# Finishing the key searches of an expert layer during its first sixteen expert pairs, in a scratch row shared with their activations

## The chip, the cores and the metric

The kernel runs on one core of a Trainium2 chip. A core has a matrix engine (TensorE, PE in the profile), three elementwise engines (VectorE or DVE, ScalarE or ACT, GpSimd or POOL) and SyncE (SP), which here issues loads. The metric is the device time of one execution in microseconds.

## The reference, cut to what matters

The model is two two-layer blocks on 256 tokens of width 1024. Each layer of the first block ends in an expert layer (`peer_ffn`) with 128 x 128 experts, and the change lies there alone; it is computed twice. For each token, 8 heads score 2 x 128 keys, the best 16 of each half are combined, and the best 16 of the 256 sums pick the experts:

```python
q = (xt @ wq).reshape(T, PEER_HEADS, 2, PEER_HALF)
s = jnp.einsum('thpd,hpkd->thpk', q, subkeys).astype(F32)
s1, i1 = lax.top_k(s[:, :, 0], PEER_TOPK)
s2, i2 = lax.top_k(s[:, :, 1], PEER_TOPK)
cand = (s1[..., :, None] + s2[..., None, :]).reshape(T, PEER_HEADS, PEER_TOPK * PEER_TOPK)
...
top_s, pos = lax.top_k(cand, PEER_TOPK)
idx = jnp.take_along_axis(cand_idx, pos, axis=-1)
gate = jax.nn.softmax(top_s, axis=-1)
...
act = jax.nn.gelu(jnp.einsum('td,thkd->thk', xb, ub).astype(F32), approximate=False)
return jnp.einsum('thk,thkd->td', (gb * act).astype(vb.dtype), vb)
```

## The kernel before

**Tiling.** The 256 tokens are two tiles of 128 (`tt` = 0, 1). There are 16 rows of 128 keys (`c` = 0 to 15: 8 heads, 2 halves). The kernel doesn't gather experts: it computes all 128 x 128 activations densely, 128 experts (a unit `c`) at a time, then multiplies them by gates that are zero except for the chosen experts.

**A unit.** `unit` (line 284) loads 512 KB of weights on SP's queue, ScalarE casts the high part `whi` (line 277), VectorE subtracts for the low part `wlo` (line 279), and `fm_unit` (line 302) runs 24 matmuls: high by high, high by low of the tokens, low by high. There are 4 buffers of raw weights, 3 of `whi`, 2 of `wlo`. Two units share one of four large PSUM banks; `divide` (line 444, VectorE) scales the bank into SBUF.

**The stages of `peer`**, in program order:

1. The scores stage: `peer_q` makes queries of 16 units in 8 pairs. After each pair `scores` scales them, runs 8 matmuls against the keys (line 1016), copies the scores to `s`, and traces the searches of these two key rows for both token tiles (32 in a layer).
2. A search (`top_keys`, lines 1031 to 1035, all on VectorE): the best 8 of 128 (MAX8), their indices (a load and FIND_INDEX8), a copy `w` without them (a load and MATCH_REPLACE8), the next best 8, and their indices. Only the last three steps touch `w`, a tile with one buffer.
3. The activations: `u_pair(c)` for c = 0, 2, ... 126 runs two units of `peer_u`, scales them and takes the Gelu on ScalarE (line 1051), into one of three tiles `H`: c < 48, 48 to 111, from 112. The second of these takes the one buffer of tag `late` over from `X`, which holds queries, scores, keys and the scratch space of `top_experts`.
4. `top_experts` (lines 1135 to 1208, almost all VectorE): from the best keys `v` and `ix` to expert indices and gates. It is traced after the pair c = 46 and ahead of the pair c = 48.
5. `gate_block` n (lines 1053 to 1076, 32 of them, 8 tokens each) is traced after the pair c = 48 + 2n: one-hot products on VectorE, 16 matmuls, and two multiplications into `H` (line 1074). Buffers of the one-hots allow two blocks at a time.
6. `peer_v`: the gated activations times the second weights (line 1117).

**What sets the order.** A planner writes each engine's queue before the run. An instruction's number is its place in the program, and `later(n)` adds n to it; among the instructions that are ready by the planner's clock, an engine's queue takes the lowest number first. In the run each queue is worked off in that order. A tile gets a buffer of its tag when its first writer is placed, and gives it back after its last reader. In `later(10000)` the searches have a number behind everything else of the layer, so they fill whatever time VectorE has. The transposes of `top_experts` are numbered as of pair c = 34.

Of the kernel before, what the change touches and what calls it, by code (L numbers as in the profile page):

```python
# [9 lines left out]
F32 = mybir.dt.float32  # L10
# [5 lines left out]
AF = mybir.ActivationFunctionType  # L16
# [5 lines left out]
P = 128  # L22
T = 256
NT = 2
# [180 lines left out]
class Kern:  # L205
# [771 lines left out]
    def peer(self, l):  # L977
        nc = self.nc
        TOP = 8
        with ExitStack() as es:  # L980
# [11 lines left out]
            s = X[:, 4096:8192].rearrange("p (t c k) -> p t c k", t=NT, k=P)  # L992
# [8 lines left out]
            with self.pool("peer_x") as px, ExitStack() as ek:  # L1001
                pk = ek.enter_context(self.pool("peer_k"))
                xT, _, divide = self.turned(self.h, f"norm_ffn{l}", px, "xT")

                raw = self.wr.tile([P, 1024], F32, tag="wraw", name="wraw")
                nc.sync.dma_start(raw, self.d("c_keys"))
                nc.vector.tensor_copy(keys, raw.rearrange("p (k t) -> p k t", t=TOP))
                nc.sync.dma_start(sk, self.d(f"peer_k{l}").rearrange("p a b -> p (a b)"))

                def scores(j, ps, m):  # L1010
                    divide(q[:, j:j + 2], ps)
                    pss = self.bank([P, NT, 2, P])
                    for n in range(2):
                        for tt in range(NT):
                            c = j + n
                            nc.tensor.matmul(pss[:, tt, n], q[:, c, tt * P:tt * P + P], sk[:, c * P:c * P + P],
                                             start=True, stop=True)
                    nc.scalar.copy(s[:, :, j:j + 2], pss)
                    with self.later(10000):
                        for tt in range(NT):  # L1020
                            for c in range(j, j + 2):
                                top_keys(tt, c)


                LOW = -3.0e38
                v = [pk.tile([P, 16, 16], F32, name=f"v{tt}") for tt in range(NT)]
                ix = [pk.tile([P, 16, 16], U32, name=f"ix{tt}") for tt in range(NT)]

                def top_keys(tt, c):
                    src, w = s[:, tt, c], pk.tile([P, P], F32, tag="w", name="w")  # L1030
                    nc.vector.max(v[tt][:, c, 0:8], src)
                    nc.vector.max_index(ix[tt][:, c, 0:8], v[tt][:, c, 0:8], src)
                    nc.vector.match_replace(w, v[tt][:, c, 0:8], src, LOW)
                    nc.vector.max(v[tt][:, c, 8:16], w)
                    nc.vector.max_index(ix[tt][:, c, 8:16], v[tt][:, c, 8:16], w)
                self.fm_proj(xT, f"peer_q{l}", range(16), scores)
                U = self.d(f"peer_u{l}")

                def u_pair(c):
                    if c == EARLY:  # L1040
                        H_.append(big.tile([P, 64, T], F32, tag="late", name="H"))
                    if c == 112:
                        H_.append(big.tile([P, 16, T], F32, tag="last", name="H"))
                    ps = self.bank([P, 2, T], True)
                    for j in range(2):
                        hi, lo = self.unit(U[c + j])
                        self.fm_unit(ps[:, j], hi, lo, xT)
                    i = (c >= EARLY) + (c >= 112)
                    hv = H_[i][:, c - FROM[i]:c - FROM[i] + 2]
                    divide(hv, ps)  # L1050
                    nc.scalar.activation(hv, hv, AF.Gelu)  # L1051

                def gate_block(oh, n):

                    t0 = n * TOP
                    bc = lambda a: a[:, None, t0:t0 + TOP].to_broadcast([P, P, TOP])
                    o2, og = hot[:, n % 2, 0], hot[:, n % 2, 2:4]

                    o1 = hot[:, n % 2, 1].rearrange("p k t -> p (k t)").rearrange("p (a k b) -> p a k b", a=4, b=2)
                    nc.vector.tensor_tensor(o2, keys, bc(i2T), op=ALU.is_equal)  # L1060
                    i1 = i1T[:, t0:t0 + TOP].rearrange("p (a b) -> p a b", b=2)
                    nc.vector.tensor_tensor(o1, keys[:, None, :, 0:2].to_broadcast([P, 4, P, 2]),
                                            i1[:, :, None, :].to_broadcast([P, 4, P, 2]), op=ALU.is_equal)
                    for k in range(2):
                        nc.vector.tensor_tensor(og[:, k], o2, bc(gT[:, k]), op=ALU.mult)  # L1065
                    late = oh.tile([P, P - EARLY, TOP], F32, tag="late", name="late")
                    for b in range(0, TOP, 4):
                        ps = self.bank([P, 4, P])
                        for t in range(4):
                            for k in range(2):  # L1070
                                nc.tensor.matmul(ps[:, t], og[:, k, :, b + t], o1[:, (b + t) // 2, :, t % 2], start=k == 0, stop=k == 1)
                        ps = ps.rearrange("p t c -> p c t")
                        hv = H_[0][:, :, t0 + b:t0 + b + 4]
                        nc.vector.scalar_tensor_tensor(hv, ps[:, 0:EARLY], 1.0 / GS, hv, op0=ALU.mult, op1=ALU.mult)
                        nc.scalar.activation(late[:, :, b:b + 4], ps[:, EARLY:], AF.Copy, scale=1.0 / GS)
                    nc.scalar.dma_start(G[n].rearrange("p (c t) -> p c t", t=TOP), late)

                for c in range(0, EARLY, 2):
                    if c == 34:
                        at = self.tc.cur_priority  # L1080
                    u_pair(c)
                self.top_experts(v, ix, X[:, 0:4096], pk, i1T, i2T, gT, at)
                ek.close()
                with self.pool("peer_oh", 2) as oh:
                    n = 0
                    for c in range(EARLY, 128, 2):
                        u_pair(c)
                        while n < T // TOP and 2 * n < c + 2 - EARLY:
                            gate_block(oh, n)
                            n += 1  # L1090
# [771 lines left out]
```

## Time and profile before

| | us |
|---|---|
| median of 3 runs | 3558.74 (3556.2 to 3559.95) |
| the profiled execution | 3559.58 |
| its span, first to last instruction | 3557.8 |
| TensorE busy | 3475.5 (98%) |
| VectorE busy | 2472.9 (70%) |
| ScalarE busy | 1780.6 (50%) |

Times in a profile count from the span's start. In the first expert layer the scores stage runs from about 357 to 414, the activations to 819; in the second they are some 1085 us later. An engine is busy while an instruction of it is being worked on; a matmul's end is modelled, and TensorE's matmuls overlap each other, so a full TensorE row means that it did not wait, not that it is at its peak. An arrow in a row names what ended the idle time before an instruction.

### The profile page before, as it was taken

What the parts mean: (1) busy time and instruction counts of PE and PEld (TensorE: products, weight loads), DVE (VectorE), ACT (ScalarE), POOL (GpSimd) and SP (SyncE); (2) the same over time, 40 slices, a digit from 0 to 9 for tenths busy, and PEclk for the clock granted to TensorE, in tenths of its full rate; (3) what the DMA queues carried; (4) which work ended last, traced back from release to release, by engine and by line L of the source; (5) the groups of instructions that cost most, each with busy time, mean ns of one, the idle gap of its engine ahead of it and who ended that gap; (6) DMA issues with size and microseconds to landing.
All of it is one profiled execution on the core that took longest, in us unless ns stands there. A gap on an engine that the chain in (4) does not pass through costs nothing. (4 is left out here: it accounts for less than half of the span.)

```text
span 3557.8 us, 59377 instructions
## 1 busy us (share of the span) xinstructions
PE 3475.5 (98%) x23428; PEld 3153.5 (89%) x23428; DVE 2472.9 (70%) x4292; ACT 1780.6 (50%) x2670; POOL 73.8 (2%) x93
## 2 busy tenths in 40 slices
PE   8999999999999999999999999999999999999898
PEld 8888999998888888999998888898898898987797
DVE  7655998977655755899987655665765665657664
ACT  5644454554444854445554444544523544444543
POOL 0000000000000000000000000000001000000000
PEclk9999999999999999999999999999998999999999
DMA  4444556668665544556667756556502455553355
GB/s 159 154 139 151 156 184 196 202 199 288 206 189 189 177 135 148 162 182 189 202 203 262 235 188 189 175 185 193 160 20 77 148 195 176 184 199 115 115 185 163
DMA packets 176832, 620.57 MB, mean 174 GB/s; under 512 B 19868, under 2 KB 20636, under 8 KB 175784
## 3 DMA queue, kind: packets, MB, share of 16 engines
q1 hardware_dynamic: 164000, 584.00, 51.9%
q10 hardware_dynamic: 12552, 32.78, 2.5%
q8 instruction: 183, 3.00, 0.3%
q14 instruction: 97, 0.79, 0.1%
HBM read 594.68 MB, written 22.02 MB: 173 GB/s over the span
## 5 line engine op out<-in xcount | busy, mean ns | idle before, releaser
L279 DVE TENSOR_TENSOR wlo<-wraw,whi 128x1024 fp32r<-128x1024 f32 x1058 | 1290.9, 1221 | 589.8 <-PE ps L1117 249.4
L277 ACT CAST whi<-wraw 128x1024 fp32r<-128x1024 f32 x1058 | 1108.4, 1050 | 1108.5 <-PE ps L302 380.5
L302 PE MATMUL ps<-xT_hi,whi 128*128 128x256 f32 x4432 | 651.1, 284 | 2.9 <-ACT xT_hi L393 2.9
L302 PE MATMUL ps<-xT_hi,wlo 128*128 128x256 f32 x4432 | 645.5, 283 | 5.9 <-DVE wlo L279 5.8
L302 PE MATMUL ps<-xT_lo,whi 128*128 128x256 f32 x4432 | 649.5, 284 | 1.1 <-DVE xT_lo L394 0.8
L302 PEld LDWEIGHTS ps<-xT_hi,wlo 128*128 128x128 f32 x4432 | 576.9, 189 | 9.9 <-DVE wlo L279 8.4
L302 PEld LDWEIGHTS ps<-xT_hi,whi 128*128 128x128 f32 x4432 | 577.5, 189 | 6.3 <-ACT xT_hi L393 5.0
L302 PEld LDWEIGHTS ps<-xT_lo,whi 128*128 128x128 f32 x4432 | 577.7, 189 | 3.5 <-DVE xT_lo L394 1.7
L1117 PE MATMUL ps<-whi,gh 128*128 128x512 f32 x2048 | 520.4, 395 | 1.1 <-DVE gh L1110 1.0
L1117 PEld LDWEIGHTS ps<-whi,gh 128*128 128x128 f32 x2048 | 384.4, 188 | 94.5 <-DVE gh L1110 2.8
L1117 PE MATMUL ps<-wlo,gh 128*128 128x512 f32 x1024 | 280.6, 395 | 0.0
L1117 PEld LDWEIGHTS ps<-wlo,gh 128*128 128x128 f32 x1024 | 192.6, 188 | 45.9
L1051 ACT ACTIVATE H<-H 128x512 f32<-128x512 f32 x128 | 81.1, 633 | 139.8 <-DVE H L444 139.5
L444 DVE TENSOR_TENSOR H<-ps,row 128x512 f32<-128x512 f32 x128 | 88.1, 688 | 73.8 <-PE ps L302 73.8
L290 PE MATMUL ps<-whi,aT_hi 128*128 128x512 f32 x352 | 138.9, 395 | 0.0
L292 PE MATMUL ps<-whi,aT_lo 128*128 128x512 f32 x352 | 138.9, 395 | 0.0
L291 PE MATMUL ps<-wlo,aT_hi 128*128 128x512 f32 x352 | 138.8, 394 | 0.0
L444 DVE TENSOR_TENSOR gu<-ps,row 128x512 f32<-128x512 f32 x88 | 60.9, 692 | 109.3 <-PE ps L302 109.3
L1110 DVE TENSOR_TENSOR gh<-H,gh 128x256 fp32r<-128x256 f32 x256 | 106.9, 418 | 1.9 <-ACT gh L1109 1.6
L1109 ACT CAST gh<-H 128x256 fp32r<-128x256 f32 x256 | 102.5, 401 | 0.0
L1065 DVE TENSOR_TENSOR hot<-hot,gT 128x1024 f16<-128x1024 f16 x128 | 82.2, 681 | 0.0
L292 PEld LDWEIGHTS ps<-whi,aT_lo 128*128 128x128 f32 x352 | 66.3, 188 | 15.5
(636 smaller groups left out, 3995.1 us busy)
## 6 DMA issues: line engine op xcount, KB each, us to landing
wraw<-in_peer_u_dram SPq DMA_DIRECT2D x256, 512.0 KB, 3.7
wraw<-in_peer_v_dram SPq DMA_DIRECT2D x256, 512.0 KB, 4.2
wraw<-in_ff_g_dram SPq DMA_DIRECT2D x88, 512.0 KB, 3.7
wraw<-in_ff_u_dram SPq DMA_DIRECT2D x88, 512.0 KB, 3.3
wraw<-in_ff_d_dram SPq DMA_DIRECT2D x88, 512.0 KB, 4.2
G<-late ACTq DMA_DIRECT2D x64, 320.0 KB, 3.8
g<-G SPq DMA_DIRECT2D x64, 320.0 KB, 5.1
wraw<-in_peer_q_dram SPq DMA_DIRECT2D x32, 512.0 KB, 3.6
```

Of the source, the lines that this page charges most:

```text
L277: nc.scalar.copy(hi, src)
L279: nc.vector.tensor_sub(lo, src, hi.bitcast(F32))
L290: mm(out, a[0], b[0], start=start, stop=False)
L291: mm(out, a[0], b[1], start=False, stop=False)
L292: mm(out, a[1], b[0], start=False, stop=stop)
L302: self.nc.tensor.matmul(out, w[n][0][:, k * P:k * P + P], w[n][1][:, k], start=i == 0, stop=i == 3 * kc - 1)
L444: return dst, lambda tt: r[:, tt:tt + 1], lambda out, ps: nc.vector.tensor_tensor(out, ps, row.to_broadcast([P, ps.shape[1], T]), op=ALU.mult)
L1051: nc.scalar.activation(hv, hv, AF.Gelu)
L1065: nc.vector.tensor_tensor(og[:, k], o2, bc(gT[:, k]), op=ALU.mult)
L1109: nc.scalar.copy(gh, src)
L1110: nc.vector.tensor_sub(gl, src, gh.bitcast(F32))
L1117: nc.tensor.matmul(acc[tt][nb], a[:, tt * P:tt * P + P], w[:, nb * 512:nb * 512 + 512], start=c == 0 and w is hi and a is gh, stop=c == 12 ...
```

## The change

The searches are no longer traced in `scores` with `later(10000)`. They are traced after the pair c for c = 0, 2, ... 30 (key row c // 2, both token tiles) with `later(100)`, which is a little under two pairs' worth of numbers. The scratch tile is twice as wide (both token tiles side by side), and in these sixteen pairs the second half of the activation passes through a tile of the same tag: scaled into `g`, Gelu from `g` into `H`. So `scale` and Gelu are each two instructions of half the width. The tag `w` still has one buffer; in program order its users are g of pair 0, searches 0, g of pair 2, searches 1, and so on.

```diff
                     nc.scalar.copy(s[:, :, j:j + 2], pss)
-                    with self.later(10000):
-                        for tt in range(NT):
-                            for c in range(j, j + 2):
-                                top_keys(tt, c)
...
-                def top_keys(tt, c):
-                    src, w = s[:, tt, c], pk.tile([P, P], F32, tag="w", name="w")
+                def scratch_():
+                    return pk.tile([P, 1, T], F32, tag="w", name="w")
+
+                def top_keys(tt, c, w):
+                    src = s[:, tt, c]
...
-                    divide(hv, ps)
-                    nc.scalar.activation(hv, hv, AF.Gelu)
+
+                    if c < 32:
+                        g = scratch_()
+                        divide(hv[:, 0:1], ps[:, 0:1])
+                        divide(g, ps[:, 1:2])
+                        nc.scalar.activation(hv[:, 0:1], hv[:, 0:1], AF.Gelu)
+                        nc.scalar.activation(hv[:, 1:2], g, AF.Gelu)
+                    else:
+                        divide(hv, ps)
+                        nc.scalar.activation(hv, hv, AF.Gelu)
...
                     u_pair(c)
+                    if c < 32:
+                        w = scratch_()
+                        with self.later(100):
+                            for tt in range(NT):
+                                top_keys(tt, c // 2, w[:, 0, tt * P:tt * P + P])
                 self.top_experts(v, ix, X[:, 0:4096], pk, i1T, i2T, gT, at)
```

## Rows read from the trace of the kernel before

**Rows 1.** The page, busy time and share of the span of each engine.

```profile
PE 3475.5 (98%) x23428; PEld 3153.5 (89%) x23428; DVE 2472.9 (70%) x4292; ACT 1780.6 (50%) x2670; POOL 73.8 (2%) x93
```

**Rows 2.** Stretches: us; busy time (instructions) per engine; clock; DMA share; GB/s.

```profile
357.50:414.50 57.00, 53.49 (x438) 51.95 (x437) 53.37 (x223) 21.05 (x24) 0.00 (x0) 1.00 0.48 148
431.00:543.00 112.00, 110.59 (x920) 109.36 (x919) 108.49 (x265) 55.42 (x64) 0.00 (x0) 1.00 0.58 180
543.00:560.00 17.00, 17.00 (x145) 17.00 (x145) 13.19 (x17) 8.08 (x10) 0.00 (x0) 1.00 0.60 188
560.00:775.00 215.00, 215.00 (x2016) 213.67 (x2015) 193.97 (x277) 110.10 (x158) 0.00 (x0) 1.00 0.66 202
775.00:819.00 44.00, 44.00 (x374) 44.00 (x373) 23.00 (x23) 21.54 (x25) 0.00 (x0) 1.00 0.63 188
1645.00:1860.00 215.00, 215.00 (x2016) 213.68 (x2015) 193.81 (x277) 110.27 (x158) 0.00 (x0) 1.00 0.65 202
```

**Rows 3.** Waits of the whole run (us, times, longest), then timelines of VectorE and TensorE.

```profile
PE ps L1016 <- DVE X L444: 7.0, 14, 0.6
...
368.87 0.67 DVE L444 TENSOR_TENSOR X<-ps,row 128x512 f32<-128x512 f32 x1
...
369.60 1.16 PE L1016 MATMUL ps<-X 128*128 128x128 f32 x8 [0.47 <-DVE X L444]
```

**Rows 4.** Timeline of VectorE at the end of the scores stage: start us, us, instruction.

```profile
411.77 0.28 DVE L1031 MAX8 v<-X 128x8 f32<-128x128 f32 x1
411.96 0.08 DVE L1033 MATCH_VALUE_LOAD w<-v,X 128x8 f32 x1
...
412.22 0.08 DVE L1032 MATCH_VALUE_LOAD ix<-v,X 128x8 f32 x1
...
412.49 0.28 DVE L1034 MAX8 v<-w 128x8 f32<-128x128 f32 x1
```

**Rows 5.** Timeline of TensorE in an earlier stage (the mLSTM heads), cut.

```profile
180.57 0.39 PE L290 MATMUL ps<-whi,yA_hi 128*128 128x512 f32 x1
...
181.73 1.90 PE L768 MATMUL ps<-va,e 128*128 128x257 f32 x8
...
183.56 1.15 PE L754 MATMUL ps<-r_R,sel 4*128 4x128 f32 x8
...
186.77 0.39 PE L290 MATMUL ps<-whi,yA_hi 128*128 128x512 f32 x1
...
189.56 0.59 PE L768 MATMUL ps<-va,e 128*128 128x257 f32 x2
189.99 1.03 PE L774 MATMUL ps<-ca,q 128*128 128x257 f32 x4
```

**Rows 6.** One stretch by line, VectorE alone: line 279, then line 444.

```profile
431.00:543.00 112.00, 46.19 (x39) 1.00 0.58 180
...
431.00:543.00 112.00, 12.96 (x19) 1.00 0.58 180
```

**Rows 7.** Timeline of VectorE: scalings of c = 30 and 46, top_experts' last line between.

```profile
507.99 0.69 DVE L444 TENSOR_TENSOR H<-ps,row 128x512 f32<-128x512 f32 x1 [0.72 <-PE ps L302]
...
543.09 0.28 DVE L1208 TENSOR_TENSOR gT<-X,gT 128x128 f16<-128x128 f32 x1
...
554.65 0.69 DVE L444 TENSOR_TENSOR H<-ps,row 128x512 f32<-128x512 f32 x1 [1.52 <-PE ps L302]
```

**Rows 8.** The page, groups by line: busy, mean ns of one; idle before, releaser.

```profile
L1051 ACT ACTIVATE H<-H 128x512 f32<-128x512 f32 x128 | 81.1, 633 | 139.8 <-DVE H L444 139.5
L444 DVE TENSOR_TENSOR H<-ps,row 128x512 f32<-128x512 f32 x128 | 88.1, 688 | 73.8 <-PE ps L302 73.8
L1110 DVE TENSOR_TENSOR gh<-H,gh 128x256 fp32r<-128x256 f32 x256 | 106.9, 418 | 1.9 <-ACT gh L1109 1.6
```

**Rows 9.** Stretches of a later stage, columns as in rows 2.

```profile
2660.00:2680.00 20.00, 19.10 (x171) 17.24 (x169) 10.29 (x19) 3.08 (x7) 7.27 (x12) 0.91 0.00 1
2680.00:2700.00 20.00, 20.00 (x86) 17.36 (x86) 5.75 (x12) 1.97 (x5) 0.00 (x0) 0.50 0.00 1
```

## Prediction, made before the changed kernel ran

> **What bounds the kernel now.** I read the page's busy line first: TensorE is busy for 98% of the span [rows 1], so a change pays only where it takes away or adds TensorE idle time. Next came the table of stretches around the changed code in the first of the two expert layers [rows 2]. In the scores stage (first row) TensorE loses 3.5 us of 57 while VectorE is busy for 53.4. From 431 to 543 VectorE is full (108.5 of 112) and TensorE idles 1.4. From 543 to 819 TensorE idles not at all, and VectorE has 3.8, 21.0 and 21.0 us free in the three rows. The second layer repeats this (last row against the fourth), so I work out one layer and double it.
>
> The scores stage's loss has one cause: the score matmuls wait for the scaled queries [rows 3]. That pair's last matmuls start until about 368, yet the scaling of line 444 starts at 368.87, the moment VectorE ends a search instruction, and the scores follow at 369.60. Over both layers it is 7.0 us in 14 waits.
>
> **Part 1, can the searches still run early?** The change sets when the searches run only if the scratch row is handed out in program order: searches number c then wait for activation c, and activation c+1 for searches c. Otherwise the planner would run them in VectorE gaps of the scores stage, as now. The trace shows the answer in another place [rows 5]. The four small PSUM buffers share one tag too. Line 754's second batch needs only data that exist before 177, and its program position is ahead of the output projection (line 290). Yet TensorE runs line 290 at 180.57, and 754 only at 183.56, after line 768, whose buffers come before it in the program. Again at 186.77: line 290 runs, while line 774, whose operands are ready, waits until line 768 has taken the buffer ahead of it (189.56, 189.99). Two buffers at least were free each time. So buffers of a tag go out in program order, and I take it that the scratch row does likewise.
>
> One search is five steps: by start times MAX8 0.19, replace with its load 0.26, index with its load 0.27, MAX8 0.19 [rows 4], and a second index 0.27: 1.18 us, 32 of them 38 us a layer. The first two steps (0.46, together 15 us) don't touch the row and can still run in the scores stage. The other three (0.72, together 23 us) are now tied to the sixteen pairs c = 0 to 30, two searches a pair.
>
> **Part 2, the scores stage.** VectorE's work there falls by some 20 us, so line 444 starts when TensorE is done. Bounds: nothing (a first step still stands ahead of it) to all 7.0 us; I take 6 for both layers: a step that is still ahead costs at most 0.3 of each 0.5, and with a third of the queue's time free there rarely is one. The 1.4 us of TensorE idle between 431 and 543, about as much in the second layer, I count as 2 more: **-8 us**.
>
> **Part 3, the first sixteen pairs.** A pair costs TensorE 5.7 us (its scalings are at 507.99 and 554.65, eight pairs apart, 5.83 with small extras [rows 7]). VectorE's share is 3.07 us: 46.19 + 12.96 us for 39 lines 279 and 19 lines 444 [rows 6], over 19.25 pairs. Added are 1.44 us of search steps and the split scaling, at most 2 x 0.418 - 0.688 = 0.15 [rows 8]. Sum 4.7 of 5.7. ScalarE's two half-width Gelus cost at most one more 0.633; it is half idle. Each pair's replace now waits for a Gelu of ScalarE, and behind it in VectorE's queue stands the next pair's line 279, for which TensorE waits. One prepared unit and 1 us of VectorE slack per pair cover that. If they didn't, a wait of up to 0.6 (one Gelu) in 16 pairs would be 10 us a layer. I take 1 a layer, from the first end, as that idle is spread: **+2 us**.
>
> **Part 4, what comes after: the stall.** The row c = 30 is scaled at 507.99 now, so some 3 us earlier then, 505; with its Gelus and the last three steps of two searches the searches end near 508. Only then may top_experts begin (line 1154 reads all of v). It needs VectorE for: 108.49 busy from 431 to 543 [rows 2], less 46.19 and 12.96, less about 4 for remaining search steps and first gate pieces: **45 us**. Now it is done at 543 (its last line, 1208, starts at 543.09 [rows 7]), ahead of the pair c = 48.
>
> Pair c = 46 ends near 554.65 - 4 = 551. From 508 to 551 are 43 us, the eight pairs ahead of top_experts in the program take 8 x 3.07 = 24.6, so 18 of its 45 fit and **27 are left** at the start of pair 48. Pairs from 48 on and all gate blocks come after top_experts in the program, so its ready instructions go first, and TensorE gets no wlo. It has prepared work of about 4 us (a unit and the next one's hi part). Later pairs let VectorE catch up: 21.0 us free in the row from 560, over 2016 matmuls at 64 to a pair with its gate block, so 0.67 us in each of 31.5 pairs; two such pairs pass while it lasts, 1 us. Stall: 27 - 4 - 1 = **22 us a layer, 44 in all**.
>
> A second wait points the same way. The H tile for c = 48 to 111 takes the buffer of X, which top_experts uses to its last line. Until then no pair from 48 on can be scaled, and the four large PSUM banks hold four pairs. Even if those pairs' wlo slipped through freely (8 x 1.18 = 9.4 us), top_experts would end at 551 + 27 + 9.4 = 587, while TensorE ran dry at 551 + 4 x 5.7 = 574: 13 us at least. With a remainder of 20 instead of 27 (some of top_experts interleaving better), 6. At the other end, no cover and 3 us more remainder: 30. I take 22, as the priorities speak for the upper half.
>
> **Sum.** 3559.6 (the profiled execution: span 3557.8 and 1.8 around it; 0.8 above the median of the runs shown, so the difference carries over) - 8 + 2 + 44 = 3597.6, against the median **3597**.
>
> **Rivals.**
> (a) *The remainder hides in VectorE's free time.* Between 543 and 819 it has 3.8 + 21.0 + 21.0 = 45.8 us free, more than 27. If the order let the pairs' line 279 go ahead of top_experts and the gates, only the gain would be left: 3559.6 - 8 = 3552, faster. It decides at 4 us of stall a layer, where -8 is eaten up. For it speaks the row from 775, half empty; against it the program order and the buffer of X, which bound the stall from below. The Trainium skill (Perfetto Trace Analysis, Identifying the Most-Contended Engine) says to rank engines by occupancy and work on the highest; by that rule VectorE at 70% would give no loss, this rival's time. The rows of 431 to 543 show why I don't follow it: VectorE is the fuller engine there.
> (b) *The row isn't handed out in turn.* The searches then run where they do now, and only the split remains: 3560. Rows 5 speak against it.
> (c) *A partial stall*: small instructions of top_experts leave gaps, 6 to 13 us a layer: 3559.6 - 8 + 2 + 2 x 8 = 3570.
> (d) *TensorE's clock falls in the stall.* It can: at 2680 the granted clock is 0.50 (1.2 of 2.4 GHz), after a stretch in which TensorE was busy for 19.1 of 20 us, and 86 matmuls run where 171 did [rows 9]. Two pairs' matmuls (14 us) at half rate, half of it under the stall, add 7 a layer: 3612. The Trainium skill (TensorE: Matmul & The Clock Gate, Part 1) says that the array's clock is halved unless the engine has been active of late; by it this would be the likelier case. I keep it low because a clock that falls while TensorE waits costs little.
>
> **Chances.** Forecast 0.70 (3580 to 3622), (a) 0.06, (b) 0.08, (c) 0.10, (d) 0.06. The range for 8 in 10 runs from 3564 (c with the smallest stall) to 3625 (30 us a layer, or d). A measurement of this kernel tells apart about 0.2%, 7 us. Slower: forecast, (d) and most of (c), 0.82. Within: (b), the rest of (c) and half of (a), 0.13. Faster 0.05.
>
> **What would show it.** Right: no MATCH_REPLACE8 in the scores stage and two in each of the pairs 0 to 15; line 1016's waits gone; line 1208 near 580 to 600 instead of 543; TensorE waiting for line 279 between 550 and 600 by some 20 us a layer; VectorE at its limit there. The forecast falls if MATCH_REPLACE8 still runs ahead of 414 (b), if TensorE's idle there is below 4 us (a), or if the loss lies in pairs 0 to 15, where VectorE would stand at replace waiting for ScalarE (part 3).

## The result and the profile after

The changed kernel takes 3594.5 us (median; 3591.0 to 3597.4) against 3559.3 for the kernel before, run beside it: ratio 1.0101, 95% interval 1.0089 to 1.0113, so 35 us slower. The forecast was 3597. Its profiled execution took 3594.8 with a span of 3593.1, 35.3 above the span before.

The page's busy line of the changed kernel, to be held against [rows 1]:

```profile
PE 3487.0 (97%) x23428; PEld 3164.0 (88%) x23428; DVE 2474.1 (69%) x4324; ACT 1785.2 (50%) x2702; POOL 73.6 (2%) x93
```

VectorE's work is the same to 1.2 us, and the matmuls are the same 23428. What changed is when VectorE works, and that shows in the stretches of the first expert layer. Columns: stretch; its length, then the busy time (and instructions) of TensorE, of its weight loads, of VectorE, ScalarE and GpSimd; TensorE's granted clock; DMA share; GB/s.

```profile
357.50:414.50 57.00, 57.00 (x478) 56.60 (x477) 41.26 (x125) 23.08 (x28) 0.00 (x0) 1.00 0.53 160
...
431.00:505.00 74.00, 74.00 (x626) 74.00 (x625) 58.18 (x185) 37.02 (x52) 0.00 (x0) 1.00 0.64 186
505.00:543.00 38.00, 36.34 (x306) 36.10 (x305) 37.94 (x111) 19.68 (x22) 0.00 (x0) 1.00 0.57 175
543.00:560.00 17.00, 10.32 (x84) 9.94 (x83) 17.00 (x86) 3.92 (x5) 0.00 (x0) 0.93 0.19 60
560.00:600.00 40.00, 31.98 (x220) 30.31 (x219) 38.65 (x59) 14.27 (x20) 0.00 (x0) 0.77 0.39 114
```

The kernel before, in the same cut where [rows 2] has another one:

```profile
431.00:505.00 74.00, 72.75 (x603) 71.74 (x602) 73.86 (x216) 34.06 (x40) 0.00 (x0) 1.00 0.57 174
505.00:543.00 38.00, 37.84 (x319) 37.63 (x319) 34.62 (x50) 21.36 (x24) 0.00 (x0) 1.00 0.60 193
560.00:600.00 40.00, 40.00 (x377) 39.75 (x376) 36.96 (x53) 20.44 (x30) 0.00 (x0) 1.00 0.63 201
```

**The gain.** The scores stage has no TensorE idle time left, the waits of line 1016 are gone [rows 3], and VectorE is free there for 15.7 us of 57. So it is in the pairs up to 505 (58.18 of 74, where it was full). The timeline of VectorE in the changed kernel shows the first pair with its halves and the tied steps, a later pair's scaling, that of c = 30, the start of top_experts (line 1157), the scaling of c = 46, top_experts' last line (1220, line 1208 of before) and the scaling of c = 48 (start, duration, engine, line; in brackets the idle time ahead and what ended it):

```profile
415.42 0.42 DVE L444 TENSOR_TENSOR H<-ps,row 128x256 f32<-128x256 f32 x1 [0.68 <-PE ps L302]
415.76 0.41 DVE L444 TENSOR_TENSOR w<-ps,row 128x256 f32<-128x256 f32 x1
416.09 1.22 DVE L279 TENSOR_TENSOR wlo<-wraw,whi 128x1024 fp32r<-128x1024 f32 x1
417.58 0.09 DVE L1032 MATCH_VALUE_LOAD w<-v,X 128x8 f32 x1 [0.28 <-ACT H L1055]
417.66 0.28 DVE L1032 MATCH_REPLACE8 w<-v,X 128x128 f32<-128x128 f32 x1
...
432.50 0.42 DVE L444 TENSOR_TENSOR H<-ps,row 128x256 f32<-128x256 f32 x1 [1.23 <-PE ps L302]
...
500.86 0.42 DVE L444 TENSOR_TENSOR H<-ps,row 128x256 f32<-128x256 f32 x1 [1.04 <-PE ps L302]
...
505.24 0.28 DVE L1157 CAST fx<-ix 128x256 f32<-128x256 uint32 x1
...
548.75 0.68 DVE L444 TENSOR_TENSOR H<-ps,row 128x512 f32<-128x512 f32 x1
...
580.69 0.27 DVE L1220 TENSOR_TENSOR gT<-X,gT 128x128 f16<-128x128 f32 x1
...
581.16 0.67 DVE L444 TENSOR_TENSOR H<-ps,row 128x512 f32<-128x512 f32 x1
```

Line 1032 is the replace: the first one of the layer stands behind the first pair's Gelu (line 1055 of ScalarE), none in the scores stage. The scaling of c = 0 starts at 415.42 instead of 420.49, that of c = 30 at 500.86 instead of 507.99 [rows 7]: 7.1 us gained. In the second layer the way from the first scaling of the scores stage to that of c = 30 shrinks by 7.4 us, so it is about 14 in both.

**The loss.** top_experts begins at 505.24 (but for 0.8 us of small sums, line 1166, that ran earlier) and VectorE is full from there to 585. TensorE's waits from 505 to 606 in the changed kernel (waiting instruction <- what released it: us in total, times, longest):

```profile
PE ps L302 <- DVE wlo L279: 7.3, 2, 6.7
PE ps L1213 <- DVE ii L1200: 5.0, 2, 3.4
PE ps L1213 <- DVE ii L1194: 2.1, 1, 2.1
PE ps L1078 <- DVE hot L1072: 1.9, 2, 1.1
```

That is 16.3 us, half of it not where I had put all of it: line 1213 are top_experts' transposes, which stand early in TensorE's queue, with the pairs' matmuls behind them. And the clock fell. Stretches of the changed kernel, cut where the granted clock changed, columns as above:

```profile
553.00:557.00 4.00, 0.00 (x0) 0.00 (x0) 4.00 (x35) 0.00 (x0) 0.00 (x0) 1.00 0.00 0
558.00:564.00 6.00, 4.61 (x21) 4.62 (x22) 6.00 (x12) 2.65 (x3) 0.00 (x0) 0.50 0.29 87
565.00:567.00 2.00, 0.00 (x0) 0.00 (x0) 2.00 (x4) 0.00 (x0) 0.00 (x0) 1.00 0.00 0
568.00:574.00 6.00, 5.28 (x23) 4.99 (x24) 6.00 (x8) 1.05 (x1) 0.00 (x0) 0.50 0.27 87
575.00:578.00 3.00, 0.44 (x2) 0.20 (x2) 3.00 (x4) 0.00 (x0) 0.00 (x0) 1.00 0.00 0
579.00:584.00 5.00, 4.45 (x28) 4.45 (x29) 5.00 (x10) 3.13 (x4) 0.00 (x0) 0.50 0.36 105
585.00:590.00 5.00, 4.99 (x48) 4.77 (x48) 3.65 (x7) 2.43 (x3) 0.00 (x0) 1.00 0.40 154
```

TensorE stood idle for 6.68 us ahead of 559.39, and meanwhile its granted clock went from 1.00 to 0.50 (1.2 of 2.4 GHz). One group of eight matmuls shows what that means: 2.08 us, where such a group takes 1.11 at full clock (the timeline of the run with top_experts behind the pairs, below).

```profile
559.39 2.08 PE L302 MATMUL ps<-xT_hi,wlo 128*128 128x256 f32 x8 [6.68 <-DVE wlo L279]
```

Counted in matmuls: from 543 to 600 it did 304, which take 304 / (522 / 57) = 33.2 us at the pace of before (522 in 57 us, from [rows 2] and the row above). So 23.8 us are lost there and 1.5 between 505 and 543, some 25 a layer, of which 16 are idle time and 9 half clock. 2 x 25.3 - 14 = 36.6, against the 35.3 measured. The distance between equal instructions agrees: from the first scaling of the first scores stage to that of the second it is 1085.1 us before (362.12 to 1447.25) and 1103.4 now (362.50 to 1465.92), 18.3 more, although 7.5 are gained up to the scaling of c = 30: 25.8 are lost behind it.

### The profile page after: what moved, and what is told of

Read it like the earlier page. It is cut to its first block, busy times and chain, and to the rows that moved or that the text cites. A ratio compares the mean times of both kernels' runs of the same rounds, so it can differ in the third digit from the quotient of the medians.

```text
span 3593.1 us, 59403 instructions
## 1 busy us (share of the span) xinstructions
PE 3487.0 (97%) x23428; PEld 3164.0 (88%) x23428; DVE 2474.1 (69%) x4324; ACT 1785.2 (50%) x2702; POOL 73.6 (2%) x93
## 5 line engine op out<-in xcount | busy, mean ns | idle before, releaser
L279 DVE TENSOR_TENSOR wlo<-wraw,whi 128x1024 fp32r<-128x1024 f32 x1058 | 1290.5, 1220 | 590.1 <-PE ps L1129 252.6
L444 DVE TENSOR_TENSOR H<-ps,row 128x512 f32<-128x512 f32 (+1 forms) x128 | 79.6, 622 | 89.7 <-PE ps L302 89.6
L1058 ACT ACTIVATE H<-H 128x512 f32<-128x512 f32 x96 | 60.8, 633 | 89.3 <-DVE H L444 89.2
L1078 PE MATMUL ps<-hot 128*128 128x128 f16 x1024 | 82.2, 232 | 3.7 <-DVE hot L1072 3.7
```

The costliest lines, as they stand in the source:

```text
L279: nc.vector.tensor_sub(lo, src, hi.bitcast(F32))
L444: return dst, lambda tt: r[:, tt:tt + 1], lambda out, ps: nc.vector.tensor_tensor(out, ps, row.to_broadcast([P, ps.shape[1], T]), op=ALU.mult)
```

## The experiments

**Theory (late start):** the searches, tied to sixteen pairs, end at 505; top_experts starts then, and what VectorE can't finish by pair 48 is lost one for one. Rivals: the split activation costs; the new place of the searches costs; the early place of the transposes costs; the order (top_experts ahead of the pairs' weights) costs; the low clock costs by itself. Each ratio below is to runs of the kernel before that were taken beside that kernel, with its 95% interval.

### The split alone

On the kernel before, whose searches stay as they were (shortened):

```
+ if c < 32:
+     g = pk.tile([P, 1, T], F32, tag="g1", name="g1")
+     divide(hv[:, 0:1], ps[:, 0:1]);  divide(g, ps[:, 1:2])
+     Gelu(hv[:, 0:1], hv[:, 0:1]);    Gelu(hv[:, 1:2], g)
```

> The kernel before with one part of the change alone: in the pairs c = 0 to 30 scaling and Gelu are split into two halves, the second by way of a scratch row of its own; the searches stay as they were, free to run in the scores stage. Late-start theory (the loss comes from top_experts beginning late, since the searches are tied to the pairs): the split costs VectorE at most 0.15 us a pair and nothing is late, so 3555 to 3565. Rival, the split activation is what costs (each half waits on the other engine): most of the 35 us stays, 3580 to 3595.

Measured: 3558.3 us, ratio 0.9999 (0.9990 to 1.0008). The split costs nothing that shows. That rival falls.

### The same place, a row of its own

On the changed kernel; the searches stay in the pairs and keep their numbers:

```
- g = scratch_()
+ g = pk.tile([P, 1, T], F32, tag="g1", name="g1")
...
- w = scratch_()
...
- top_keys(tt, c // 2, w[:, 0, tt * P:tt * P + P])
+ top_keys(tt, c // 2, pk.tile([P, P], F32, tag="w0", name="w0"))
```

> The changed kernel with its searches at the same place in the program and with the same numbers, but on a scratch row of their own, so that no search waits for an activation. Late-start theory: the searches run early again, in VectorE's gaps of the scores stage, top_experts ends near 543 and the stall at pair 48 is gone, and the waits of line 1016 come back: 3555 to 3566. Rival, the new place and number of the searches cost, not the shared row: 3585 to 3597, and MATCH_REPLACE8 still absent from the scores stage.

Measured: 3558.4 us, ratio 0.9998 (0.9990 to 1.0007). Only the sharing of the row is undone, and the whole 35 us are gone. The scores stage is again what it was, here in the stretches and the waits of TensorE of this kernel:

```profile
357.50:414.50 57.00, 53.43 (x438) 51.87 (x437) 53.33 (x223) 21.16 (x25) 0.00 (x0) 1.00 0.51 149
...
543.00:560.00 17.00, 17.00 (x144) 16.95 (x143) 12.83 (x15) 7.97 (x9) 0.00 (x0) 1.00 0.68 190
560.00:600.00 40.00, 40.00 (x378) 39.78 (x378) 37.24 (x54) 20.22 (x30) 0.00 (x0) 1.00 0.64 206
```

```profile
PE ps L1016 <- DVE X L444: 3.6, 7, 0.6
PE ps L302 <- DVE wlo L279: 1.3, 3, 0.5
```

So it isn't the place in the program either: with the searches free, the planner runs them in the scores stage, and line 1016 waits as before. The row handed out in turn is what holds them back.

### How many pairs are tied

Three kernels, each the changed one with another end of the taking of turns (code shortened). Two key rows a pair, done after eight pairs:

```
- if c < 32:
-     w = scratch_()
-     ... top_keys(tt, c // 2, ...)
+ if c < 16:
+     for r in (c, c + 1):
+         w = scratch_()
+         ... top_keys(tt, r, ...)
```

> The changed kernel with the turn-taking finished in eight pairs: two key rows a pair for c = 0 to 14. VectorE then has 3.1 + 2.9 + 0.15 = 6.1 us of work in a pair of 5.7, so TensorE may lose up to 0.4 x 8 = 3 us a layer there. Late-start theory: the searches end near 465 instead of 505; by pair 48 (about 549) VectorE has 83 us, less 14.5 pairs at 3.13, so 38 of top_experts' 45 us fit instead of 18; about 7 are left, of which prepared work covers 4: stall 2 to 4 us a layer, clock full. 3559.6 - 13 + 6 + 6 = 3558, range 3545 to 3568. Rival, the wait follows from handing the row back and forth as such, or from the early number of top_experts' transposes: still 3580 or more.

Rows 0 to 7 free in the scores stage, 8 to 15 tied to eight pairs (and, in the next one, rows 0 to 3 free and 4 to 15 tied to twelve):

```
  nc.scalar.copy(s[:, :, j:j + 2], pss)
+ if j < 8:
+     with self.later(10000): ... top_keys(tt, c, pk.tile([P, P], F32, tag="w0", name="w0"))
...
- if c < 32:  ... top_keys(tt, c // 2, ...)
+ if c < 16:  ... top_keys(tt, 8 + c // 2, ...)
```

> The changed kernel with key rows 0 to 7 free to be searched in the scores stage (scratch row of their own), and only rows 8 to 15 tied, one to each of the pairs c = 0 to 14. Late-start theory: as with two rows a pair the tied searches end near 463, and VectorE isn't overfull in those pairs: stall 2 to 4 us a layer; half of the gain ahead of the pairs stays (-6): 3559.6 - 6 + 6 = 3559, range 3546 to 3566. If the loss went with each handing over of the row rather than with the late end, half of it would be left: 3576.

> The changed kernel with key rows 0 to 3 free to be searched in the scores stage and rows 4 to 15 tied, one to each of the pairs c = 0 to 22: twelve pairs instead of sixteen or eight. Late-start theory: the tied searches end near 484; until pair 48 (549) VectorE has 65 us, less 11 pairs at 3.13, so 30 of top_experts' 45 us fit; 15 are left, less 5 of cover, 10 us a layer: 3560 - 10 + 20 = 3570, range 3562 to 3578. Rival, the loss comes only with the last pairs (any end ahead of c = 32 is early enough): 3550 to 3558.

| tied | us | ratio (95%) |
|---|---|---|
| no pair (row of its own) | 3558.4 | 0.9998 (0.9990 to 1.0007) |
| eight pairs, two rows each | 3561.8 | 1.0011 (1.0003 to 1.0020) |
| eight pairs, one row each | 3557.8 | 1.0000 (0.9991 to 1.0009) |
| twelve pairs | 3576.0 | 1.0052 (1.0039 to 1.0066) |
| sixteen pairs (the change) | 3594.5 | 1.0101 (1.0089 to 1.0113) |

From eight to twelve pairs 18.2 us, from twelve to sixteen 18.5 (by the ratios 18.5 and 17.4). That is the size the theory gives: a pair of 5.70 us leaves VectorE 5.70 - 3.07 = 2.6 us for top_experts, so four pairs later take 4 x 2.6 = 10.5 us a layer from it, 21 in both; four more key rows out of the scores stage give back a quarter of 14, 3.5; net 17.5. (For twelve pairs I had expected 3570, 6 too low.) Even the early end wins nothing. With one row a pair TensorE still idles 2.7 us in the scores stage and 2.5 from 505 to 560. With two rows a pair VectorE is short in those pairs; the stretches of that kernel:

```profile
431.00:505.00 74.00, 72.11 (x597) 70.94 (x596) 73.49 (x249) 35.28 (x45) 0.00 (x0) 1.00 0.58 172
505.00:543.00 38.00, 36.24 (x303) 36.04 (x302) 37.91 (x108) 18.85 (x21) 0.00 (x0) 1.00 0.59 179
543.00:560.00 17.00, 14.63 (x121) 14.17 (x121) 17.00 (x23) 6.93 (x8) 0.00 (x0) 1.00 0.39 107
```

VectorE is full from 431 to 560, and TensorE loses 1.9, 1.8 and 2.4 us, against 1.3, 0.2 and 0 in the kernel before: 4.6 us more, about what is gained ahead of the pairs.

### The transposes' place

```
- self.top_experts(v, ix, X[:, 0:4096], pk, i1T, i2T, gT, at)
+ self.top_experts(v, ix, X[:, 0:4096], pk, i1T, i2T, gT, self.tc.cur_priority)
```

> The changed kernel with one thing altered: top_experts' transposes and the copies behind them keep the number of their own place in the program instead of that of pair 34, so they stand later in TensorE's queue. In the changed kernel 7 us of TensorE's 16 us idle time a layer lie ahead of these transposes (line 1213). Theory that VectorE's left-over work sets the loss (it is busy for 5.00 of 5 us throughout 540 to 585): the 7 us only move to the waits for wlo, 3590 to 3597. Rival, the early place of the transposes in TensorE's queue is a cause of its own: 7 us a layer come back, and some of the low clock with them, 3575 to 3582.

Measured: 3593.2 us, ratio 1.0099 (1.0083 to 1.0114): nothing comes back. TensorE now loses nothing from 505 to 543, but 16.4 us instead of 14.7 from 543 to 600; line 1213 still shows 7.2 us of waits. The idle time at the transposes is a symptom: TensorE waits for VectorE, at whichever instruction comes up first.

The same edit on the kernel with two rows a pair:

> Two key rows a pair, so that the taking of turns ends with the eighth pair, and top_experts' transposes with the number of their own place. With the turn-taking ended early VectorE has room ahead of pair 48, so here the transposes' early place could cost by itself: 2.8 us of TensorE idle a layer lay ahead of them in the kernel with two key rows a pair. If it does: 3554 to 3558. If that idle time only stands for VectorE's lag: 3559 to 3563 as there.

Measured: 3570.5 us, ratio 1.0037 (1.0024 to 1.0051), slower by 9 than with the early place: a miss for both expectations. In this kernel VectorE, which ought to be the bound, idles at 540 to 550, and its next pick on the second half of the tokens comes behind the copies of the first half:

```profile
540.00:545.00 5.00, 5.00 (x44) 5.00 (x44) 2.68 (x4) 2.73 (x3) 0.00 (x0) 1.00 0.74 229
545.00:550.00 5.00, 5.00 (x44) 5.00 (x43) 2.81 (x3) 2.17 (x3) 0.00 (x0) 1.00 0.71 213
```

```profile
550.45 0.69 DVE L444 TENSOR_TENSOR H<-ps,row 128x512 f32<-128x512 f32 x1 [1.56 <-PE ps L302]
551.06 0.28 DVE L1216 CAST i1T<-ps 128x128 f16<-128x128 f32 x1
...
551.65 1.21 DVE L1195 TENSOR_REDUCE ii<-X 128x64 f32<-128x1024 f32 x1
```

The first half's ii was ready at 512, but its transposes ran at 550.25 and the second half's first reduction into ii at 551.65, instead of 511.93 and 537.56. There is one buffer ii, so the second half can write it only when the transposes have read it; the 4.5 us of VectorE lost here, twice, are the 9 us. That the single buffer is the reason is read from code and times; I didn't try a second one.

### top_experts behind the pairs

```
- self.top_experts(...)
+ with self.later(600):
+     self.top_experts(...)
```

> The changed kernel with top_experts numbered 600 later, so that the weights of the first four or so pairs from c = 48 are prepared ahead of it, as far as the buffers let them. Theory that the order (top_experts first) carries the stall and X's buffer with four PSUM banks only bounds it from below: TensorE runs dry about 570 instead of 555 and again works at about 587 to 590: 13 to 17 us a layer instead of 24: 3570 to 3582. Rival, X's buffer alone sets it, whatever the order: 3590 to 3597. Rival, the order is all of it: below 3565.

Measured: 3595.8 us, ratio 1.0108 (1.0092 to 1.0123): the same as the change, as the rival has it. My theory of the order falls. TensorE did run on with the next four pairs, and then stood for longer. Its timeline in this kernel:

```profile
570.13 1.11 PE L302 MATMUL ps<-xT_hi,wlo 128*128 128x256 f32 x8
585.00 0.47 PE L1214 MATMUL ps<-ident,ii 128*128 128x128 f32 x1 [13.76 <-DVE ii L1201]
...
595.93 0.69 PE L1214 MATMUL ps<-ident,ii 128*128 128x128 f32 x2 [7.90 <-DVE ii L1195]
```

The weights of those pairs took VectorE time that top_experts lacked afterwards; its last line starts at 597.64 instead of 580.69. The order decides where TensorE stands, not for how long. What holds the pairs back until then, X's buffer or VectorE's full queue, isn't told apart by this run: both end with top_experts' last line, and I tried no kernel that gives H a buffer of its own.

### Less work on VectorE

```
- pick(ii[:, 1], pf, i16, ALU.is_equal, fx[:, :, 1])
+ nc.vector.tensor_copy(ii[:, 1], pf)
```

> The changed kernel with a part of top_experts left out: its second pick (the three lines that find the second key, 2 x 3 passes of 1.22 us on each half of the tokens) is replaced by one copy of 0.28, so the experts chosen are others. That is 2 x (7.3 - 0.3) = 14 us of VectorE less a layer, with the searches tied to sixteen pairs as before. Theory that VectorE's left-over work at pair 48 is the loss, one for one: 3594.5 - 28 = 3566, range 3560 to 3573. Rival, the low clock of TensorE or the taking of turns in the pairs costs by itself: at most half of it comes back, 3578 or more.

Measured: 3564.9 us, ratio 1.0021 (1.0011 to 1.0031). 14 us less of VectorE work a layer bring 29.6 us by the medians (28.5 by the ratios), 14 to 15 a layer; top_experts' last line starts at 566.55 instead of 580.69. One for one, with the taking of turns and the split untouched. The clock recovers as well. That last line, and the stretch that had 0.77 in the changed kernel:

```profile
566.55 0.28 DVE L1220 TENSOR_TENSOR gT<-X,gT 128x128 f16<-128x128 f32 x1
...
560.00:600.00 40.00, 38.72 (x340) 37.51 (x341) 39.83 (x65) 20.53 (x30) 0.00 (x0) 0.93 0.63 191
```

### Was there a gain to be had in the scores stage?

On the kernel before, the score matmuls and the copy behind them are numbered 30 or 60 later, so that they stand one or two units behind in TensorE's queue:

```
+ with self.later(30):
      pss = self.bank([P, NT, 2, P])
      ... nc.tensor.matmul(pss[:, tt, n], ...)
      nc.scalar.copy(s[:, :, j:j + 2], pss)
```

> The kernel before with one thing altered: the score matmuls of line 1016 are numbered 30 later, so they stand one unit (24 matmuls) behind in TensorE's queue and find the scaled queries ready although VectorE searches first. Searches stay free to run in the scores stage. If the waits of line 1016 (7.0 us in 14 in the kernel before) were the whole of what tying the searches won there: 3559 - 7 = 3552 (3549 to 3554). If they only move to another wait (VectorE is busy for 53 of 57 us there): 3556 to 3561.

> As the run with 30, but numbered 60 later: two units behind. The same 3549 to 3554 if the waits were only a matter of the place in TensorE's queue; more than there if the scores, and with them searches and top_experts, come too late: 3555 or more.

Measured: 3558.0 (1.0004; 0.9995 to 1.0013) and 3555.6 (0.9994; 0.9985 to 1.0002): no difference that can be told from none. TensorE's waits from 357 to 640, with 30 and then with 60 (the kernel before has 3.5 for line 1016 [rows 3] and 1.2 for line 279):

```profile
PE ps L302 <- DVE wlo L279: 2.9, 8, 0.6
PE ps L1017 <- DVE X L444: 1.9, 4, 0.7
```

```profile
PE ps L302 <- DVE wlo L279: 4.0, 9, 0.8
```

The waits for the scaled queries fall to 1.9 and then to none (line 1017 here is line 1016 of before), and waits for the weights' low parts take their place. VectorE is short of time from 357 to 543 as a whole, and a wait removed at one instruction comes back at another. None of the kernels tried is measurably faster than the kernel before.

## Why the prediction was right, step by step

**Part 1, the row goes out in program order:** right. The first replace is at 417.58, behind the first pair's Gelu, and a row of its own undoes everything. That line 1154 reads all of v was not quite so: only one of its four sums needs the last key row in full, and 0.8 us of top_experts ran ahead of 505.

**Part 2, -8:** the mechanism was right, the size too small. I took the idle time of line 1016 at 0.5 us a wait. From the first scaling of the scores stage to that of the first expert pair it is eight pairs: 362.12 to 420.49 before, 7.30 us each, and 362.50 to 415.42 now, 6.62 each. That is 5.4 us, though TensorE's idle time fell by only 3.5. The rest was inside its busy time: 438 matmuls in 53.49 busy us before, 478 in 57.00 now, 8.19 and 8.39 a us. The better reading would have been the distance between equal instructions, not the idle time. VectorE's work in these 57 us fell by 12 (53.37 to 41.26), not by some 20. The scalings, in the kernel before and then in the changed one (that of 415.42 stands above):

```profile
362.12 0.69 DVE L444 TENSOR_TENSOR X<-ps,row 128x512 f32<-128x512 f32 x1 [1.69 <-PE ps L302]
...
420.49 0.68 DVE L444 TENSOR_TENSOR H<-ps,row 128x512 f32<-128x512 f32 x1
```

```profile
362.50 0.69 DVE L444 TENSOR_TENSOR X<-ps,row 128x512 f32<-128x512 f32 x1 [1.69 <-PE ps L302]
```

**Part 3, +2:** too careful. The pairs run at exactly 5.70 us, VectorE idles 1.2 us in each, and the replace waits for the Gelu once (0.28, pair 0). Against 5.83 before, that is another 2 us a layer gained. Parts 2 and 3 together: -6 forecast, -14 measured.

**Part 4, 22 us a layer:** right in place and nearly in size (some 25), partly by luck. Searches ended at 505 instead of 508. Added up from the start of each instruction to the start of the next, top_experts takes 50.7 us of VectorE in the changed kernel, not 45. I had subtracted the pairs' lines by their durations, which run into the next instruction (the scaling of 415.42 lasts 0.42 us, the next one starts after 0.34). But up to c = 46's scaling there fitted 24.6 of it, not 18, mostly because three of the low parts of the eight pairs were ready at 505. So 25.4 were left, where I had 27: two errors that cancel. The 31.5 us from c = 46's scaling to top_experts' end hold these 25.4, three low parts (3.4) and gate pieces (2.8: one each of lines 1067 and 1069, two of 1072). The gate pieces, which need only the first half of the tokens, I left out. The errors of parts 2 and 3 (8 us too little gain) and of this one (5 too little loss) largely cancel, which is why 3597 came so near.

**The second bound and the reason for the upper half:** wrong. I said that if the pairs' low parts went ahead, TensorE would lose 13 us instead of 22, and took the upper value because the priorities favour top_experts. With the order turned round the time is the same. Letting the pairs go first moves the moment when TensorE runs dry from 553 to 571, but top_experts' end moves as well, for VectorE's work up to there is a fixed sum. It needed no argument about priorities.

**Rival (a), hidden in free time:** no, in either order. X's buffer ties the scaling of the pairs from 48 on to top_experts' end (its last line starts at 580.69, the scaling of c = 48 at 581.16). The Trainium skill's rule of ranking engines by occupancy (Perfetto Trace Analysis, Identifying the Most-Contended Engine) gave this rival; here the engine at 69% of the span (70 in [rows 1]) sets 25 us a layer, so over the whole span the trace disagrees with the rule. Over the stretch from 505 to 543 the rule finds it: VectorE is busy for 37.94 of 38 us there, TensorE for 36.34.

**Rival (d), the clock:** it fell, as the Trainium skill (TensorE: Matmul & The Clock Gate, Part 1) says of an engine that hasn't been active of late, and the trace agrees: 1.00 to 557 and 0.50 from 558, in a pause of 6.68 us. I had put 7 us a layer on top for it. It cost nothing that shows: leaving out 14 us of VectorE work gave back 14 to 15, though much of the 9 us of half clock went with it, and with top_experts behind the pairs TensorE idles 22 us between 543 and 600 and works little at half clock, for the same time. So while VectorE sets the end, slower matmuls seem only to fill the waiting; no run held the clock at full in this place, so this stays an inference from those two.

**What the text named as signs:** all seen, except that only 7.3 of the 16 us of idle time stand at line 279; 7.1 stand at line 1213 and 1.9 at the gate matmuls of line 1078.

**Two sums that don't come out:** the top of the range, 3625, isn't reached by what it names: 30 us a layer make 3613, (d) makes 3612, and only both together 3627. And of the chances, slower at 0.82 takes 0.06 of (c), which leaves 0.15 for within and 0.03 for faster, not 0.13 and 0.05.

## What to carry to other kernels

Two uses of one buffer tag are tied together in program order; before sharing a tag, ask what the later of the two is the first step of, and when that must be done. Where an engine is full over a long stretch, treat its work up to the next fixed point as one sum: moving it later costs the free time passed over (here 2.6 us a pair a layer), while reordering within the stretch, or removing one wait, only moves the idle time to another instruction, unless it leaves the full engine itself idle, as the late transposes did in the kernel with two rows a pair (9 us). And the size of such an effect is read better from the distance between equal instructions than from the idle time of a wait.

## What the runs showed of the hardware that was not expected

TensorE's clock did not simply stay low once it had fallen: in the changed kernel it went to and fro between its two levels (the stretches from 553 to 590 under the result). It was at 0.50 from 558 to 564 and from 568 to 574, with 21 and 23 matmuls, and at 1.00 from 565 to 567 and from 575 to 578, with none and two. Each time it rose behind a stretch of matmuls and fell again behind a pause, so that most matmuls met the low level and the pauses the high one. It was back at 1.00 from 585, behind a stretch in which TensorE was busy for 4.45 of 5 us (28 matmuls). With top_experts behind the pairs it fell later and stayed at 0.50 for 27 us, in which TensorE was busy for 7.5:

```profile
574.00:601.00 27.00, 7.53 (x57) 6.98 (x58) 25.81 (x58) 4.22 (x9) 0.00 (x0) 0.50 0.11 34
```
